# Five projection pairs of a hybrid decoder layer moved to Strassen products behind the values' stage

## The chip, the cores and the metric

The kernel runs on one core of a Trainium2 chip. The metric is the device time of one execution, in microseconds (us), taken as the median over runs; lower is better. TensorE is called PE in the profile, VectorE DVE, ScalarE ACT, GpSimd POOL and SyncE SP.

## The reference

One decoder layer works on 1024 tokens of width 1024, all in float32. The part that the change touches is the first projection and what consumes it:

```python
h = rms_norm(x, pre_mix_g[l])
proj = h @ w_in[l]
qa, ka, va, qb, kb, vb, gates = jnp.split(proj, split_at, axis=-1)
qa = apply_rope(qa.reshape(b, s, A_HEADS, 2, A_QK_DIM), cos_a, sin_a)
ka = apply_rope(ka.reshape(b, s, A_HEADS, 2, A_QK_DIM), cos_a, sin_a)
...
oa = diff_attention(qa, ka, va, lam)
...
qb = apply_rope(qb.reshape(b, s, B_GROUPS, B_HEADS, B_HEAD_DIM), cos_b, sin_b)
...
g_a, g_b = jnp.split(jax.nn.sigmoid(gates), 2, axis=-1)
mix = (g_a * ya + g_b * yb) @ w_mix_out[l]
x = x + rms_norm(mix, post_mix_g[l])
```

Attention A has 4 heads; each has two 64-wide queries and keys and is causal over all tokens (a difference of two softmaxes). Attention B has three groups of four 128-wide heads over dilated windows. The rotation of a head (`apply_rope`) takes `t1*cos - t2*sin` and `t2*cos + t1*sin` of its two halves. There are 16 gate units of 128 columns. A convolution-gated MLP follows, with two more large matrix products.

## The kernel before, in words

**Numbers.** Every float32 operand is kept as a high part (rounded to `fp32r`) and a low part (the rest). `split` (L148) makes them: ACT copies the high part (L149), DVE subtracts it from the source (L146, in `sub`). A product is three matmuls, high x high, low x high and high x low (`mm3`, L153 to L157), 128 rows deep, 128 columns of the stationary operand wide and at most 512 moving columns.

**Stages.** The transposed input stands in SBUF as `xh` and `xl` (8 blocks of 128 rows, 1024 tokens). First come the values of A and B (L445 to L653), as tokens x 2048 columns, by Strassen's scheme with seven products; sums of x are made for it (`t2`, `t3`, `t4`, and a sum that takes the place of the second half of x's first four blocks, `b12`). While the last products run, that half of x is loaded again and split (`again`, L650 to L653). The values go to DRAM through the POOL queue (`put_v`, L535). Beside it the rotation tables are made and stored in DRAM, with the row norm multiplied into them.

Then attention A begins (L907). `proj_t` (L235) projects 128 columns: it loads a unit of weights (`load_unit`, L129: two pieces of 256 KB on the SP queue, each split), and for each half of the tokens does 8 x 3 matmuls into one PSUM bank. For queries and keys the evacuation is `rotated` (L679): ACT copies the swapped blocks (L684), DVE multiplies by the two tables and adds (L685 to L687); then ACT and DVE write the high and low parts that attention uses (L730 to L744). For a gate it is `put_gate` (L248): DVE multiplies by the row norm, and the ACT queue stores it. Before head 0, one gate and head 0's projections run by themselves (L910, L911).

A head of A is eight jobs (`attend_a`, L749), one for each 128 queries: score matmuls, a minimum on DVE (L770), exponentials on ACT (L777), their difference on DVE, and later transposes (L697) and products with the values (L710, L713). Beside the jobs run *fills*: `A_FILLS` gives a string for each head, where `g` is a gate, `p` the two projections of the next A head, `P` those of the first B head, `v`, `w`, `x` and `V` loads and splits of values. `interleave` (L294) places pieces of them between the jobs by weight. Attention B (L1124) runs 12 steps of four jobs with the next step's projections as the fill, the last step with three gates (`B_GATES`). Then come the output projections, the mixing, and the MLP, whose first product is Strassen's as well (`seven`, L1437).

**Order.** Each engine and each DMA queue (SP, ACT, POOL) works in order. The order in which an engine gets its instructions is chosen by a list scheduler, from the order of the program, priorities (`tc.high_priority`) and a simulated time line; `tc.issue_after` fixes an order where it is written. Buffers are reused in turn: 18 slots of 4 KB a partition (`SLOTS`) for attention operands, six pairs of weight buffers (`slot_w`), PSUM in pools `acc` (3 banks), `pt` (2), `ps_s` (2) and `ps_o` (1).

Of the kernel before, what the change touches and what calls it, by code (L numbers as in the profile page):

```python
# [15 lines left out]
F32 = mybir.dt.float32  # L16
# [8 lines left out]
P = 128  # L25
# [24 lines left out]
START_GATES, A_FILLS, B_GATES = 1, ("gpgg", "gpvgg", "wgpgg", "xgPVgg"), 3  # L50
# [37 lines left out]
def trunk(ctx: ExitStack, tc: tile.TileContext, a, out):  # L88
# [64 lines left out]
    def mm3(o, sh, sl, mh, ml, first, last, on=False):  # L153

        nc.tensor.matmul(o, sh, mh, start=first, stop=False, skip_group_check=on)  # L155
        nc.tensor.matmul(o, sl, mh, start=False, stop=False, skip_group_check=on)  # L156
        nc.tensor.matmul(o, sh, ml, start=False, stop=last, skip_group_check=on)  # L157
# [42 lines left out]
    def halves():  # L200
        return [slice(i * 512, (i + 1) * 512) for i in range(2)]
# [20 lines left out]
    c_d = dram.tile([NF, P, S], F32, name="c_d")  # L222

# [32 lines left out]
    due, clock, marks = [], [0], {}  # L256

    @contextmanager
    def behind_marks():

        with ExitStack() as stack:
            for ins in marks.values():
                stack.enter_context(tc.issue_after(ins))
            yield

# [48 lines left out]
    rstd_row = open_pool(attn, "row", side="right").tile([P, S], F32, name="rstd_row")  # L314
    st_a = ExitStack()
# [4 lines left out]
    t2, t3, t4 = ([xw0.tile([P, 4, 512], F32R, tag=n + p, name=n + p) for p in "hl"] for n in ("t2", "t3", "t4"))  # L320
    tb = open_pool(st_v, "tb", side="right")
# [12 lines left out]

    def new_tabs():
        return [tabs.tile([P, S], F32, tag=t, name=t) for t in ("cos", "sin")]
# [17 lines left out]
    def load_tabs(first, n):  # L354

        cos, sin = new_tabs()
        for q in range(P // n):
            to = slice(q * n, (q + 1) * n)
            dma(cos[to], tab_d[0][first : first + n])
            dma(sin[to], tab_d[1 if q % 2 else 2][first : first + n])  # L360
        return cos, sin

# [11 lines left out]
    def sums_x(k, low, high):  # L374


        g1, g2 = gpre[:, k : k + 1], gpre[:, k + 4 : k + 5]
        e, o = (tb.tile([P, 2, 512], F32, tag=t, name=t) for t in ("sin", "cos"))
# [17 lines left out]
    def norm_x(m):  # L396
# [5 lines left out]
        if m < 8:  # L402
            rows_x.append(tb.tile([P, S], F32, tag=("kk", "ang", "sin", "cos")[m % 4], name="rows"))
            nc.gpsimd.dma_start(rows_x[m], a["x"][m * P : (m + 1) * P])
# [40 lines left out]
    with ExitStack() as st_y:  # L445
# [17 lines left out]
        def more_tags():  # L463

            for tag in itertools.cycle(("ang", "kk", "sin", "cos")):
                t = tb.tile([P, S], F32, tag=tag, name="raw")
# [145 lines left out]
        made, fetched, again = 12, 14, []  # L612

        places_y = {("p6", 1): (1, "a0", yv), ("p5", 1): (3, "b3", yw), ("p4", 1): (2, "b2", yw)}
        quarter.update({(q, 0): new_y(f"b{q}", yw) for q in range(1, 4)})
        for n in range(8, len(steps_v)):
# [15 lines left out]
            if n == ANGLES_AT:  # L632
                pos = [load_raw(a["positions"][sl].partition_broadcast(P), next(tags)) for sl in halves()]
                args = [tb.tile([P, S], F32, tag=n_, name=n_) for n_ in ("sin", "cos")]
# [10 lines left out]
            step_v(n)  # L645
            if k == 3 and i and p in ("p1", "p7", "p4", "p3"):
                put_v({"p1": 0, "p7": 3, "p4": 2, "p3": 1}[p], 1, p == "p1")
            if (p, i) == ("p5", 1):

                again.append(load_raw(a["xT"][k][:, 512:], next(tags)))  # L650
            if (p, i) == ("p6", 1):
                with behind_marks():
                    split_x(k, halves()[1], again[k])  # L653
    st_v.close()
    tabs = open_pool(attn, "tabs", side="right")
    cos_a, sin_a = load_tabs(64, 32)
# [22 lines left out]
    def rotated(ps, cos, sin, sl, quarter):  # L679
        t1 = rt.tile([P, 512], F32, tag="t1", name="t1")  # L680
        t2 = rt.tile([P, 512], F32, tag="t2", name="t2")
        for q in range(P // quarter):
            src, dst = slice((q ^ 1) * quarter, ((q ^ 1) + 1) * quarter), slice(q * quarter, (q + 1) * quarter)
            nc.scalar.activation(t1[dst], ps[src], AF.Copy)  # L684
# [41 lines left out]
    def proj_a(h, res):  # L726
# [3 lines left out]
        def put_q(half, sl, ps):  # L730
            t = rotated(ps, cos_a, sin_a, sl, 32)
# [5 lines left out]
        def put_k(half, sl, ps):  # L737
            t = rotated(ps, cos_a, sin_a, sl, 32)
# [8 lines left out]
        yield from proj_t(KA + h * P, put_k)  # L747

    def attend_a(h, i, ops, vs, out_sb, pair):  # L749
# [51 lines left out]
        def add(b):  # L801
            if b == 0:
                po.append(psum(F32, ps_o, "o")[:, : 2 * P].rearrange("p (n q) -> p n q", n=2))
# [50 lines left out]
    free_gates = list(range(2 * KC))  # L854
# [11 lines left out]

    def proj_b(g, h, res, between=None):
# [5 lines left out]
        def put(hi, lo):  # L873
            def evacuate(half, sl, ps):
                t = rotated(ps, *tabs_b, sl, 64).rearrange("p (i r) -> p r i", r=dil)
# [31 lines left out]
    with st_a:  # L907
        ops = [[] for _ in range(AH)]
        vs = [[] for _ in range(AH // 2)]
        run(gates(START_GATES)[0])  # L910
# [3 lines left out]
        for h in range(AH):  # L914
# [3 lines left out]
                "p": lambda: (proj_a(h + 1, ops[h + 1]), 8),  # L918
# [3 lines left out]
                "P": lambda: (proj_b(0, 0, ops_b[steps[0]]), 8),  # L922
# [27 lines left out]
    def attend_b(g, h, jj, ops, vs, sbs):  # L950
# [48 lines left out]
        def values():  # L999
            po = psum(F32, ps_o, "o")[:, : 2 * P].rearrange("p (j q) -> p j q", j=2)  # L1000
# [697 lines left out]
def layout(inp):  # L1698
# [10 lines left out]
    us = []  # L1709
    for c in plan():  # L1710
        us.append(units(w[:, c : c + P], KC, P))
# [31 lines left out]
```

## Time and profile before

| | |
|---|---|
| median of 3 runs | 1696.49 us (1695.46 to 1696.99) |
| the profiled execution | 1697.3 us, span 1695.3 us from its first to its last instruction |
| granted TensorE clock | 0.998 of full speed |
| values' stage | to about 162 us |
| gate and head 0's projections | 162 to 203 us |
| attention A | 203 to about 530 us (its minima on DVE, L770, from 208 to 503) |
| attention B | to about 875 us (its minima, L975, from 545 to 854) |
| output projections, mixing, the MLP's first plain units | to about 1117 us |
| MLP, up, by Strassen products | to about 1476 us |
| MLP, down | to the end |

How to read it: the page gives the share of the span in which each engine was busy, the chain of work that ended last, and groups of instructions by line, with the busy time, the mean duration of one in ns, and the idle time in front of them. Matmuls are pipelined, so that the durations of neighbours overlap. A line can be that of a helper. Windows give the busy time of each engine in a stretch of the span, with the number of instructions, the clock granted, the busy share of the 16 DMA engines and their rate.

### The profile page before, as it was taken

The numbers are of one execution on the slowest core, as the hardware profiler recorded it, in microseconds if no ns is written. First come the engines' busy times: TensorE is split into PE (matmuls) and PEld (weight loads), VectorE is DVE, ScalarE is ACT, GpSimd is POOL, SyncE is SP. The second block draws the span as 40 slices with busy tenths as digits, with TensorE's granted clock in tenths as the row PEclk, the third lists the DMA queues.
The fourth block names the chain that finished last, engine by engine and source line by source line (L and its number), as shares of the span: only waits on it lengthen the run. The fifth ranks groups of instructions, "written<-read, shape, count | busy, mean of one in ns | idle before, by whom it ended". The sixth has DMA issues, their size and how long they took to land.

```text
span 1695.3 us, 22960 instructions
## 1 busy us (share of the span) xinstructions
PE 1682.1 (99%) x8078; PEld 1410.0 (83%) x8078; DVE 1333.5 (79%) x2445; ACT 891.8 (53%) x1663; POOL 106.3 (6%) x174
## 2 busy tenths in 40 slices
PE   9999999999999999999999999999999999999997
PEld 7888888888888888888888888888888888888886
DVE  8795686877776766677756865899999989799967
ACT  7643575656454776666653533464444445355453
POOL 0031000000000000000123400300000000000000
PEclk9999999999999999999999999999999999999999
DMA  8677311214112213233585631132222222296524
GB/s 266 234 253 235 99 60 62 86 59 119 50 63 81 70 53 108 86 112 119 200 285 186 203 118 63 38 106 92 95 81 75 98 83 88 95 343 214 193 75 161
DMA packets 104451, 216.41 MB, mean 128 GB/s; under 512 B 12992, under 2 KB 22144, under 8 KB 104336
## 3 DMA queue, kind: packets, MB, share of 16 engines
q1 hardware_dynamic: 89296, 171.28, 30.5%
q0 software_dynamic: 10288, 35.28, 6.1%
q10 hardware_dynamic: 4752, 8.39, 1.3%
q8 instruction: 63, 1.03, 0.3%
q14 instruction: 52, 0.43, 0.1%
HBM read 167.05 MB, written 47.86 MB: 127 GB/s over the span
## 4 chain that ended last, share of the span: by engine, by line
PE 97%; DMA 2%; DVE 1%; ACT 1%; issue 0%; SPq 0%; DVEq 0%
PE acc L155 22%; PE acc L156 22%; PE acc L157 22%; PE acc L1578 3%; PE acc L1579 3%; PE acc L1577 3%; PE o L710 2%; PE pt L697 2%; PE acc L1258 2%; PE acc L1256 2%; PE acc L1257 2%; PE o L713 1%; PE s L156 1%; PE s L157 1%; PE s L155 1%; PE s L768 1%
## 5 line engine op out<-in xcount | busy, mean ns | idle before, releaser
L156 PE MATMUL acc<-xh,wlo 128*128 128x512 f32 x768 | 303.2, 395 | 0.0
L157 PE MATMUL acc<-xl,whi 128*128 128x512 f32 x768 | 303.1, 395 | 0.0
L155 PE MATMUL acc<-xh,whi 128*128 128x512 f32 x768 | 303.0, 395 | 0.0
L149 ACT ACTIVATE whi<-raw 128x512 fp32r<-128x512 f32 (+1 forms) x252 | 156.1, 626 | 170.3 <-PE acc L157 88.1
L146 DVE TENSOR_TENSOR wlo<-raw,whi 128x512 fp32r<-128x512 f32 (+1 forms) x252 | 178.8, 717 | 40.4 <-ACT whi L149 34.7
L156 PEld LDWEIGHTS acc<-xh,wlo 128*128 128x128 f32 x768 | 144.4, 188 | 27.8
L157 PEld LDWEIGHTS acc<-xl,whi 128*128 128x128 f32 x768 | 144.5, 188 | 27.5
L155 PEld LDWEIGHTS acc<-xh,whi 128*128 128x128 f32 x768 | 144.4, 188 | 27.3
L155 PE MATMUL acc<-mh,whi 128*128 128x512 f32 x400 | 155.8, 390 | 0.3 <-ACT mh L149 0.3
L156 PE MATMUL acc<-mh,wlo 128*128 128x512 f32 x400 | 155.6, 389 | 0.0
L157 PE MATMUL acc<-ml,whi 128*128 128x512 f32 x400 | 155.3, 389 | 0.0
L684 ACT ACTIVATE t<-acc 64x512 f32<-64x512 f32 (+1 forms) x160 | 94.7, 592 | 55.3 <-PE acc L157 53.3
L1454 DVE TENSOR_TENSOR u<-acc,u 128x512 f32<-128x512 f32 x133 | 91.3, 691 | 20.3 <-PE acc L157 20.1
L149 ACT ACTIVATE whi<-s 128x512 fp32r<-128x512 f32 x76 | 46.9, 627 | 102.3 <-PE acc L157 88.1
L685 DVE TENSOR_TENSOR t<-acc,cos 128x512 f32<-128x512 f32 x64 | 44.1, 690 | 67.1 <-ACT t L684 63.5
L155 PEld LDWEIGHTS acc<-mh,whi 128*128 128x128 f32 x400 | 75.1, 188 | 16.0 <-ACT mh L149 0.5
L156 PEld LDWEIGHTS acc<-mh,wlo 128*128 128x128 f32 x400 | 75.1, 188 | 15.6
L157 PEld LDWEIGHTS acc<-ml,whi 128*128 128x128 f32 x400 | 75.1, 188 | 15.5
L1578 PE MATMUL acc<-whi,wlo 128*128 128x512 f32 x220 | 77.6, 390 | 0.0
L1577 PE MATMUL acc<-whi 128*128 128x512 f32 x220 | 76.4, 389 | 0.0
L1579 PE MATMUL acc<-wlo,whi 128*128 128x512 f32 x220 | 73.2, 390 | 0.0
L777 ACT ACTIVATE s<-s,mx 128x896 f32<-128x896 f32 (+7 forms) x64 | 49.4, 772 | 36.9 <-DVE mx L770 21.0
(387 smaller groups left out, 3941.6 us busy)
## 6 DMA issues: line engine op xcount, KB each, us to landing
raw<-in_w_in SPq DMA_DIRECT2D x96, 256.0 KB, 2.9
raw<-in_w_up SPq DMA_DIRECT2D x88, 256.0 KB, 2.8
raw<-in_w_v SPq DMA_DIRECT2D x71, 256.0 KB, 4.7
raw<-c_d SPq DMA_DIRECT2D x48, 256.0 KB, 3.8
c_d<-c SPq DMA_DIRECT2D x22, 512.0 KB, 2.7
raw<-in_w_down SPq DMA_DIRECT2D x37, 256.0 KB, 4.1
v_d<-yv POOLq DMA_DIRECT2D x32, 256.0 KB, 4.5
gt_d<-gate ACTq DMA_DIRECT2D x32, 256.0 KB, 2.1
```

The lines of the kernel that those rows point to most:

```text
L146: eng.tensor_tensor(lo, src, hi.bitcast(F32), op=ALU.subtract)
L149: copy = nc.scalar.activation(hi, src, AF.Copy)
L155: nc.tensor.matmul(o, sh, mh, start=first, stop=False, skip_group_check=on)
L156: nc.tensor.matmul(o, sl, mh, start=False, stop=False, skip_group_check=on)
L157: nc.tensor.matmul(o, sh, ml, start=False, stop=last, skip_group_check=on)
L684: nc.scalar.activation(t1[dst], ps[src], AF.Copy)
L685: nc.vector.tensor_tensor(t2, ps, cos[:, sl], op=ALU.mult)
L777: exp = nc.scalar.activation(sc[c][:, :w], sc[c][:, :w], AF.Exp, bias=mx[:, c, 0:1], scale=-1.0, accum_out=den[:, c : c + 1])
L1454: nc.vector.tensor_tensor(to, made(p), x, op=ALU.add)
L1577: nc.tensor.matmul(banks[m], gh[:, tk], wh, start=f == 0, stop=False)
L1578: nc.tensor.matmul(banks[m], gl[:, tk], wh, start=False, stop=False)
L1579: nc.tensor.matmul(banks[m], gh[:, tk], wl, start=False, stop=f == NH - 1)
```

## The change

Ten of the 48 units of the projection are taken out of the attentions and done in a new stage between the values and attention A, in five pairs: the first B head's queries and keys, the last two gates, and the queries and keys of A's heads 1, 2 and 3. A pair is a product of 256 columns with the whole x, done as seven products of half the depth, half the columns and half the tokens, with the values' sums of x (`t2`, `t3`, `t4`, `b12`), which therefore stay longer. The reload of x's second half comes behind the last pair.

- *Weights.* Four sums of weight quarters are needed for a pair (`s1` to `s4`). They are made by DMAs on the POOL queue that add to their destination (`add_to`), started from a loaded quarter or from a negated copy by ACT. A pair's sums are begun up to two pairs ahead, its operands split one pair ahead.
- *Products.* `seven_q` runs p1, p4, p2, p6, p7, p5, p3; p2 goes on in p1's bank and p3 in p5's after these were read, and p3 of a pair is run behind p1 of the next. Eight PSUM banks of all pools are used in turn.
- *Rotation.* `rotate_q` multiplies the tile by both tables on DVE, and two accumulating DMAs add the swapped halves. For that the tables' signs lie differently (`load_tabs`, and `other` in `rotated`), and the columns of the three A heads are permuted on the host.
- *Storing.* `store_q` splits a tile and stores high and low parts in DRAM (`qk_d`); attention loads them into the slots it uses (`load_a`, `load_b`), by 12 DMAs for an A head and 4 for a B head. The gates go to DRAM as before, but unsplit from this stage.
- *Order.* `in_turn` fixes the order of ACT and DVE over this stage's blocks, from the last four steps of the values.
- *Attentions.* Fills become three gates a head for heads 0 to 3 with `l` and `L` for the loads; no gate runs before head 0; the last B step has two gates for three. The outputs' accumulator takes turns between `ps_o` and `acc` (`outs`).

```diff
-START_GATES, A_FILLS, B_GATES = 1, ("gpgg", "gpvgg", "wgpgg", "xgPVgg"), 3
+A_FILLS, B_GATES = ("glgg", "glvgg", "wglgg", "xgLVgg"), 2
+EARLY_GATES = 2
...
+    outs = itertools.cycle([lambda: psum(F32, ps_o, "o"), psum])
...
+    def in_turn():
+        with ExitStack() as stack:
+            for ins in tail.values():
+                stack.enter_context(tc.issue_after(ins))
+            last = nc.cur_bb.bb.instructions[-1]
+            yield
...
+                if ins.engine in (nc.scalar.engine, nc.vector.engine):
+                    tail[str(ins.engine)] = ins
...
+        pairs = [AH, len(plan()) // 2 - 1, 1, 2, 3]
...
+        def begin(src, scale=None):
+            t = sum_tile()
+            if scale:
+                nc.scalar.activation(t, src, AF.Copy, scale=scale)
+            else:
+                dma(t, src)
+            return t
+        def add_to(t, src):
+            nc.gpsimd.dma_start(t, src, accum_op=ALU.add)
+        def sums_a(n):
+            d11, d12, d21, d22 = quarters(n)
+            to = sums_q[n] = {"a11": load_raw(d11, "raw"), "s1": begin(d21), "a22": load_raw(d22, "t1"), "a12": load_raw(d12, "t2")}
+            to["s3"] = begin(to["s1"], -1.0)
+            to["s2"] = begin(to["a11"], -1.0)
+            add_to(to["s1"], d22)
+            add_to(to["s3"], d11)
+            add_to(to["s2"], to["s1"])
+        def sums_b(n):
+            _, d12, _, _ = quarters(n)
+            to = sums_q[n]
+            to["s4"] = begin(to["s2"], -1.0)
+            add_to(to["s4"], d12)
...
+            if n == len(steps_v) - 8:
+                with in_turn(), tc.high_priority(offset=60):
+                    sums_a(0)
...
+        def rotate_q(n, c, u):
+            if pairs[n] >= len(order) // 2 - KC:
+                nc.vector.tensor_tensor(u, u, rstd_row, op=ALU.mult)
+                return
+            sw = pq.tile([P, S], F32, tag="sw", name="sw", bufs=2)
+            nc.vector.tensor_tensor(sw, u, tab[1], op=ALU.mult)
+            nc.vector.tensor_tensor(u, u, tab[0], op=ALU.mult)
+            for src, dst in ((up_half, low_half), (low_half, up_half)):
+                add_to(u[dst], sw[src])
+        def store_q(n, c, u):
...
+            hi, lo = (pq.tile([P, S], F32R, tag=t, name=t, bufs=2) for t in ("qkh", "qkl"))
+            split(hi, lo, u)
...
+                for b in range(4 if head < AH else 0):
+                    to = (b % 2 * 2 + b // 2) * 32
+                    dma(qk_d[2 * head + c, i, to : to + 32], f32(t[b * 32 : (b + 1) * 32]))
...
+        for n in range(len(pairs)):
+            made_q = seven_q(n, ws_q.pop(n))
+            if n == 2:
+                tab = load_tabs(64, 32)
+            next(made_q)
+            if n:
+                next(before)
+                with in_turn():
+                    rotate_q(n - 1, 1, old[1])
+            with in_turn():
+                if n == 0:
+                    sums_a(1)
+                    sums_b(1)
+                put_w(n + 1, "a11")
+                for m, fn in ((n + 1, sums_b), (n + 2, sums_a)) if n else ((2, sums_a),):
+                    if m < len(pairs):
+                        fn(m)
+            next(made_q)
+            with in_turn():
+                if n:
+                    rotate_q(n - 1, 0, old[0])
+                put_w(n + 1, "a22", "a12")
...
+                put_w(n + 1, "s2", "s3")
...
+            old = next(made_q)
...
+                put_w(n + 1, "s1", "s4")
+                if n:
+                    store_q(n - 1, 0, last[0])
...
-        run(gates(START_GATES)[0])
         run(proj_a(0, ops[0]))
```

In `seven_q`, where `made(p, bank)` does one product's 12 matmuls:

```diff
+            m1 = made("p1")
+            copy(c11, m1)
+            yield
+            m4 = made("p4")
+            made("p2", m1)
+            m6 = made("p6")
+            add(c12, m6, c11)
+            copy(c11, m1)
+            yield
+            m7 = made("p7")
+            add(c22, m7, c12)
+            add(c21, m4, c22)
+            yield
+            m5 = made("p5")
+            add(c22, m5, c22)
+            yield us
+            made("p3", m5)
+            add(c12, m5, c12)
```

More of the change, by code (lines that the diff above doesn't have):

```diff
@@ L677, in split_values, with rotated @@
                 split(*res[-1], v)
-    def rotated(ps, cos, sin, sl, quarter):
+    def rotated(ps, cos, sin, sl, quarter, other=()):
         t1 = rt.tile([P, 512], F32, tag="t1", name="t1")
@@ L865, in trunk, with load_b @@
     tabs_b, wk_b = [], []
+    def load_b(g, h, res):
+        ops = [slot(n) for n in ("qh", "ql", "kh", "kl")]
+        res += ops
+        at = where[QB + g * 512 + h * P]
+        for n, t in enumerate(ops):
+            dma(f32(t), qk_d[at + n // 2, n % 2])
     def proj_b(g, h, res, between=None):
```

157 lines of the change are left out of this document (122 added, 35 removed).

## The prediction

> **What bounds the kernel now.** I read the page's engine shares and its chain first, then who TensorE waits for.
>
> ```profile
> span 1695.3 us, 22960 instructions
> PE 1682.1 (99%) x8078; PEld 1410.0 (83%) x8078; DVE 1333.5 (79%) x2445; ACT 891.8 (53%) x1663; POOL 106.3 (6%) x174
> ...
> PE 97%; DMA 2%; DVE 1%; ACT 1%; issue 0%; SPq 0%; DVEq 0%
> ```
> ```profile
> PE acc L155 <- ACT xh L371: 1.8, 2, 1.4
> PE pt L578 <- DVE t4l L575: 1.2, 1, 1.2
> PE acc L155 <- ACT mh L149: 0.3, 1, 0.3
> ```
>
> The chain is 97% TensorE, and TensorE's waits add up to 3.3 us, most of it before the first products. So a TensorE instruction that goes is worth its full issue interval, and everything else costs nothing until it makes TensorE wait. The interval isn't the listed mean of a matmul: those overlap. Windows restricted to the tile acc give it, and windows over all engines the load of each stage.
>
> ```profile
> 162.00:203.00 41.00, 40.77 (x180) 33.80 (x180) 4.15 (x6) 9.88 (x17) 1.00 0.41 128
> ```
> ```profile
> 90.00:128.00 38.00, 38.00 (x173) 31.52 (x172) 37.27 (x71) 13.76 (x22) 13.81 (x23) 1.00 0.83 288
> 128.00:162.00 34.00, 34.00 (x151) 28.16 (x150) 19.98 (x31) 13.56 (x23) 4.86 (x9) 1.00 0.70 218
> 203.00:280.00 77.00, 77.00 (x386) 65.20 (x385) 59.10 (x132) 47.86 (x96) 0.00 (x0) 1.00 0.21 72
> 1130.00:1480.00 350.00, 350.00 (x1546) 289.91 (x1545) 318.04 (x426) 150.23 (x203) 3.38 (x34) 1.00 0.26 88
> ```
>
> The columns are window, length, then busy time of PE, PEld, DVE, ACT and (where it works) POOL, the granted clock, DMA share, GB/s. From 162 to 203 us (a gate and head 0's projections) 180 matmuls of 512 columns take 40.77 us: 0.2265 us each, at full clock. The last row matters too: in the feed-forward Strassen stage DVE works 318 of 350 us, 91%, and TensorE is busy throughout.
>
> **Matmuls removed.** Each 128-column projection is 2 halves x 8 k x 3 = 48 matmuls, a pair 96. Strassen takes 7 products x 4 k x 3 = 84. Five pairs (a B head, two gates, A heads 1 to 3) lose 12 each: 60 x 0.2265 = 13.6 us. The other matmuls, transposes included, stay. So a new pair lasts 84 x 0.2265 = 19.0 us on TensorE, a product 2.72, the five pairs 95.1.
>
> **What the new stage asks of DVE and ACT.** Rows by form, the mean in ns behind the comma:
>
> ```profile
> L146 DVE TENSOR_TENSOR wlo<-raw,whi 128x512 fp32r<-128x512 f32 x250 | 178.0, 719 | 37.5 <-ACT whi L149 31.9 <-DMA sin<-tab_d 2.7 <-POOL gl L1225 1.2
> L149 ACT ACTIVATE whi<-raw 128x512 fp32r<-128x512 f32 x250 | 155.3, 628 | 169.4 <-PE acc L157 88.1 <-issue 22.8 <-PE acc L1578 13.3
> L1454 DVE TENSOR_TENSOR u<-acc,u 128x512 f32<-128x512 f32 x133 | 91.3, 691 | 20.3 <-PE acc L157 20.1
> L1343 DVE TENSOR_TENSOR c<-c 128x1024 f32<-128x1024 f32 x22 | 26.9, 1224 | 0.1
> L146 DVE TENSOR_TENSOR vl<-vperm,vh 128x1024 fp32r<-128x1024 f32 x16 | 19.4, 1222 | 2.6 <-ACT vh L149 2.6
> L149 ACT ACTIVATE vh<-vperm 128x1024 fp32r<-128x1024 f32 x16 | 16.5, 1048 | 0.1
> ```
>
> A head's pair costs DVE 7 weight splits (7 x 0.719 = 5.0), 5 additions out of PSUM (3.5), 4 multiplications by the tables (4 x 1.224 = 4.9) and 2 splits for storing (2.4): 15.8 of 19.0 us, 83%. ACT: 7 splits 4.4, two copies 1.2, three negated copies 1.9, two stores 2.1: 9.6 us. The gate pair asks less. This is below the 91% that costs nothing at 1130 to 1480 us, so I price it at zero. If that cover fails it is because DVE or ACT, which work in order, stand waiting for a DMA; that is priced next.
>
> **The accumulating DMAs.** The trace has none. Per head's pair the change puts 8 on the POOL queue: four for weight sums (s1, s3, s2, s4; s2 waits for s1, s4 for s2) and four for the rotation (two per tile). Nearest are the plain 256 KB transfers from the same queue, at the busiest place of the kernel, and the weight loads.
>
> ```profile
> L535 POOL DMA_DIRECT2D v_d<-yv x32: 540/541/902, 107.2 to 163.9; - x32
> DMA to landing us min/median/max: 2.7/4.5/8.3
> ```
> ```profile
> raw<-in_w_v SPq DMA_DIRECT2D x71, 256.0 KB, 4.7
> ```
>
> Let L be the time from issue to landing. Below, the plain one: 2.7 to 4.5 us. Above, twice the plain one, because a destination has to be read as well: 9 us at the median, 16.6 at the slowest. Less than nothing is excluded, as these DMAs replace no transfer on TensorE's path. I take 7 to 9, nearer to twice the median, since the stage is as full of transfers as 90 to 128 us. Three places feel L.
> - Pair 0. Its sums are issued eight steps (8 x 2.72 = 22 us) before the values end, and s4 is used 6 products later: no wait at any L up to about 10.
> - Pair 1. Its sums begin about when pair 0 does. s2 is ready at 4.7 + 2L + 1.3 (load, two accumulations, split) and is used after ten products, at 27.2. TensorE waits 2L - 21: nothing at 9, 12 us at 16.6. Behind ACT's waiting negation of s2 queue later splits, so I take 1 us at L = 8.
> - Stores of a rotated tile. DVE's and ACT's order is fixed by hand here, so a store that waits for its rotation holds everything behind it: the next pair's negated copies, and through them the POOL queue, which in turn waits for s1 before the next rotation. That loop lasts about 2L + 4 us (two landings, issues and copies) against 19.0: free up to L = 7.5. It closes only once, while pair 1 is multiplied, since pair 2's slot has the gates, which have no rotation, and the last two slots begin no new sums. At L = 8 to 9 it costs 1 to 3 us; I take 1.5.
>
> **Bytes.** A head's pair moves 7 weight pieces, one sum to another, 4 rotations and 2.1 MB of stored high and low parts: 20 pieces of 0.262 MB, 5.2 MB in 19 us, or 275 GB/s. The row of 90 to 128 us carried 288 with TensorE never idle, and the page's slices of 42 us go up to 343:
>
> ```profile
> GB/s 266 234 253 235 99 60 62 86 59 119 50 63 81 70 53 108 86 112 119 200 285 186 203 118 63 38 106 92 95 81 75 98 83 88 95 343 214 193 75 161
> ```
>
> Counted over all five pairs (the gates' has 12 pieces), tables (2.1) and the reload of x (1.0), 27 MB go into 95.1 us plus the 21.7 of head 0's projections (96 x 0.2265) that follow: 234 GB/s. So bytes alone don't bind; they make L long. [...]
>
> **What only moves.** The reload and split of x's second half (four pieces of SP's, eight operations like a split, 5.4 us on two engines) goes behind the last p5; it is awaited by the second half of head 0's queries, one product and 24 matmuls later, 8.2 us: nothing, and if its cover is gone 1 or 2 us once. The tables' loads come earlier on SP, the first during pair 0, whose rotation is a pair later. POOL's mask for A stands behind the accumulations, but is wanted only after head 0's projections: nothing.
>
> **The attention of A.** What leaves each of the windows like 203 to 280: two units, 96 matmuls, 21.7 us of TensorE, with their DVE work of 4 splits (2.9), 12 rotation operations and 12 splits of 64 rows:
>
> ```profile
> L685 DVE TENSOR_TENSOR t<-acc,cos 128x512 f32<-128x512 f32 x64 | 44.1, 690 | 67.1 <-ACT t L684 63.5 <-PE pt L697 2.0 <-PE o L713 1.3
> L744 DVE TENSOR_TENSOR l<-t,k 64x512 fp32r<-64x512 f32 x32 | 21.9, 684 | 1.0 <-ACT k L741 0.4
> ```
>
> 12 x 0.690 + 12 x 0.684 + 2.9 = 19.4 us. So DVE goes from 59.1 of 77 (77%) to 39.7 of 55.3 (72%): attention alone isn't denser on DVE than before. What is lost is filling: 3 gates behind eight jobs, where there were 3 gates and 2 projections. Bounds: a gain of 1 us (the second accumulator bank for the outputs) to a loss of 3 us a head; I take 0.5 in all, as the gates depend on nothing and can be placed anywhere. The twelve loads a head (3.1 MB in 55 us, 57 GB/s on top of 72) sit on SP's queue ahead of the next gate's weights and wait for slots that the head before has left by then: nothing. With two gates for three, the last B step keeps 21.7 us of filling: nothing.
>
> **Sum.** -13.6 + 1 + 1.5 + 0.5 = -10.6 us. The profiled execution took 1697.3 us, 2.0 more than its span; that gives 1686.7. The median of the runs, 1696.5, is 0.8 lower: 1685.9, say 1686.
>
> **Rivals.**
> [...]
> - *Attention runs dry.* If a head's chain (scores, DVE's minimum, exponentials, transposes) shows through with less filling, at 2 us a head: 8 us instead of 0.5, with the rest 1693.5. Against: DVE at 72% only.
> - *Slower: the POOL queue.* If L passes about 12.5, the three places together cost what was saved: pair 1 waits 4, the loop 10. At the upper bound 16.6: pair 1 12 us, the loop 18, two late stores 3 each, about 36 less a few that overlap, 30: 1696.5 - 13.6 + 30 = 1713. For: the queue works in order and nothing here shows an accumulation. Against: 4.5 us at the median with DVE 37.27 of 38 us busy. [...]
> - *It doesn't do what it says.* Should matmuls be kept, their count wouldn't fall; the loop bounds leave little room.
>
> **How the numbers follow.** About 0.2% (3.4 us) is what a measurement of this kernel can tell from no change: faster is below 1693.1, slower above 1699.9. Forecast (1682.5 to 1690) 0.64; transfers bind 0.13, half of it below 1693.1; attention dry 0.07, a little more than half below; slower 0.12; the rest, 0.04, no change. Faster: 0.64 + 0.065 + 0.045 = 0.75; slower 0.12; same 0.13. The range starts at 1682, all gain and a little more, and runs to 1699: the two middle rivals are inside, about 0.12 are above and some 0.06 below.
>
> **What would show it.** TensorE's count 60 lower, and its total shorter by 13 to 14 us of matmul intervals. In the new stage TensorE's idle should be 1 to 4 us, behind ACT's or DVE's splits near the start of pairs 1 and 2; accumulations land at 7 to 9 us; DVE stands at about 83%. A head's attention lasts 55 us. I am wrong if accumulations land later than 12 us, if the DMA share in the stage is 0.95 and TensorE waits for weight splits all through it, or if a head lasts more than 58 us.

## The result and the profile after

The kernel after takes 1753.88 us (median of 4 runs, 1749.96 to 1759.28), the kernel before 1696.74 us beside it (4 runs): a ratio of 1.0339, with a 95% interval of 1.0309 to 1.0368. It is 57 us slower where 10.6 us of gain were forecast. The profiled execution took 1759.3 us, the longest of the four and 62.0 more than that of before. The page of after:

```profile
span 1757.5 us, 23054 instructions
PE 1695.6 (96%) x8018; PEld 1412.0 (80%) x8018; DVE 1334.9 (76%) x2419; ACT 864.9 (49%) x1615; POOL 138.3 (8%) x210
PEclk9999999899999999999999999999999999999999
PE 77%; DMA 9%; DVE 6%; issue 3%; ACT 3%; POOL 1%; SPq 1%; DVEq 0%; ACTq 0%; POOLq 0%
```

The 60 matmuls are gone (8078 to 8018), but TensorE no longer ends the chain alone: its share fell from 97% to 77%. Three numbers give the whole difference. TensorE is idle for 1757.5 - 1695.6 = 61.9 us, before 1695.3 - 1682.1 = 13.2: 48.7 more. Its busy time grew by 13.5 us although 13.6 us of matmuls went, so the rest takes 27.1 us longer; the mean granted clock fell from 0.998 to 0.984, and 1.4% of 1696, my estimate of the clock's part, is 24 of them. 48.7 + 27.1 - 13.6 = 62.2, the difference of the spans. Who TensorE waits for:

```profile
PE pt L898 <- DVE s L993: 13.9, 10, 3.4
PE s L976 <- DVE mx L979: 9.7, 10, 4.3
PE pt L156 <- DVE u L763: 8.7, 2, 6.0
PE s L156 <- DVE stat L1190: 3.2, 1, 3.2
PE acc L911 <- ACT pt L150: 2.9, 2, 1.5
```

Only the third line belongs to the new stage. The others are waits of attention A (the fourth: of B's first step) for its own softmax, which other products used to cover. Windows by stage show the same (window, length, then busy time of PE, PEld, DVE, ACT, POOL, the granted clock, DMA share, GB/s): most of the new stage, its last products and head 0's projections, the start of head 0, from the end of head 0 into head 1, from head 2 into head 3, and at the end everything from 200 to 660 us.

```profile
162.00:262.00 100.00, 93.97 (x405) 77.30 (x404) 56.50 (x73) 36.00 (x61) 25.58 (x31) 0.97 0.76 181
262.00:301.00 39.00, 35.53 (x150) 28.63 (x149) 28.94 (x40) 24.53 (x40) 4.13 (x6) 0.96 0.77 207
301.00:345.00 44.00, 27.42 (x111) 19.84 (x112) 32.99 (x79) 23.30 (x47) 0.00 (x0) 0.81 0.70 178
345.00:396.00 51.00, 50.62 (x284) 43.51 (x283) 34.16 (x106) 19.37 (x47) 0.00 (x0) 1.00 0.44 129
450.00:510.00 60.00, 55.98 (x297) 46.93 (x296) 38.50 (x116) 22.39 (x57) 0.00 (x0) 0.94 0.35 119
200.00:660.00 460.00, 419.15 (x2103) 349.75 (x2102) 301.71 (x726) 213.59 (x455) 17.16 (x25) 0.95 0.44 124
```

In the kernel before, TensorE was busy for all 460 us from 200 to 660, at clock 1.00. Here it stands still for 40.9 of them, and at a clock of 0.95, 5% of 419 us, 21 us more, go to the clock by the same estimate. The worst place is the start of head 0: 27.42 us of work in 44, at 0.81.

### The profile page after: what moved, and what is told of

Read it like the earlier page. It is cut to its first block, busy times and chain, and to the rows that moved or that the text cites. A ratio compares the mean times of both kernels' runs of the same rounds, so it can differ in the third digit from the quotient of the medians.

```text
span 1757.5 us, 23054 instructions
## 1 busy us (share of the span) xinstructions
PE 1695.6 (96%) x8018; PEld 1412.0 (80%) x8018; DVE 1334.9 (76%) x2419; ACT 864.9 (49%) x1615; POOL 138.3 (8%) x210
## 4 chain that ended last, share of the span: by engine, by line
PE 77%; DMA 9%; DVE 6%; issue 3%; ACT 3%; POOL 1%; SPq 1%; DVEq 0%; ACTq 0%; POOLq 0%
PE acc L156 17%; PE acc L157 16%; PE acc L158 16%; PE acc L1794 3%; PE acc L1792 3%; PE acc L1793 3%; PE acc L1471 2%; PE acc L1473 2%; PE acc L1472 2%; PE pt L898 2%; DMA raw<-in_w_in 2%; DMA mw<-e_d 1%; DMA s<-in_w_in 1%; DMA u<-sw 1%; PE acc L911 1%
## 5 line engine op out<-in xcount | busy, mean ns | idle before, releaser
L157 PE MATMUL acc<-xh,wlo 128*128 128x512 f32 x640 | 254.1, 397 | 0.0
L156 PE MATMUL acc<-xh,whi 128*128 128x512 f32 x640 | 253.9, 397 | 0.0
L158 PE MATMUL acc<-xl,whi 128*128 128x512 f32 x640 | 253.8, 397 | 0.0
L158 PEld LDWEIGHTS acc<-xl,whi 128*128 128x128 f32 x640 | 121.2, 189 | 23.6
L156 PEld LDWEIGHTS acc<-xh,whi 128*128 128x128 f32 x640 | 121.5, 190 | 23.2
L157 PEld LDWEIGHTS acc<-xh,wlo 128*128 128x128 f32 x640 | 121.4, 190 | 22.8
L150 ACT ACTIVATE whi<-s 128x512 fp32r<-128x512 f32 x96 | 58.7, 626 | 123.5 <-PE acc L158 100.7
L886 DVE TENSOR_TENSOR t<-acc,cos 128x512 f32<-128x512 f32 x48 | 33.2, 692 | 67.6 <-ACT t L885 63.9
L885 ACT ACTIVATE t<-acc 64x512 f32<-64x512 f32 (+1 forms) x104 | 61.6, 593 | 45.3 <-PE acc L158 42.7
L979 DVE CUSTOM_DVE_ANT_0 s<-s,mask_a 128x512 f32<-128x512 f32 (+3 forms) x96 | 52.3, 554 | 32.7 <-PE s L977 17.7
```

What stands on the lines that cost most here:

```text
L150: copy = nc.scalar.activation(hi, src, AF.Copy)
L158: return nc.tensor.matmul(o, sh, ml, start=False, stop=last, skip_group_check=on).ins
L885: nc.scalar.activation(t1[dst], ps[src], AF.Copy, scale=-1.0 if q in other else 1.0)
L979: nc.vector.tensor_tensor_reduce(out=s_sb[:, c0:c1], in0=ps, in1=mask, scale=-scale, scalar=3.0e38, op0=ALU.add, op1=ALU.min, accum_out=mx ...
```

## The experiments

Every kernel of this part is the change, or the kernel before, with the edit shown; `...` stands for lines that only go along with it. Times are medians, and ratios are set against the kernel before on the same chip. *Lost time* is how much further apart TensorE's matmuls start than the median interval of their shape in the kernel before, summed over a stretch; it holds idle time and a lower clock together. The first four asked what in the change slows attention A: the loads on SP's queue, the missing filling, the accumulating DMAs, or something else.

**The loads on another queue.**

```diff
-            dma(f32(to), src)
+            nc.gpsimd.dma_start(f32(to), src)
...
```

> The loads of the stored heads (12 for an A head, 4 for the B head) are issued from the POOL queue instead of SP's; nothing else changes. Theory S (SP's queue): these loads keep the gates' weights back, so that attention A has no other matmuls beside it; then TensorE's idle time from attention A's first scores to B's first (about 32 us after the change) falls below 10, and the kernel takes about 1725 us. Theory F (filling): twelve pieces of filling a head are too few beside eight jobs whatever the loads do; then the idle time stays within 5 us of what it is and the kernel at 1748 to 1758.

Measured: 1762.36, ratio 1.0384 (1.0368 to 1.0399). The loads no longer stand ahead of the gates' weights on SP, and nothing is gained; the time is 4 us above even the case in which filling is what lacks. The queue isn't the main cause.

**Two pairs instead of five, the old filling in A.**

```diff
-A_FILLS, B_GATES = ("glgg", "glvgg", "wglgg", "xgLVgg"), 2
+A_FILLS, B_GATES = ("gpgg", "gpvgg", "wgpgg", "xgLVgg"), 2
...
-        pairs = [AH, len(plan()) // 2 - 1, 1, 2, 3]
+        pairs = [AH, len(plan()) // 2 - 1]
...
```

> Only the first B head and the two gates go by Strassen's scheme; the projections of A's heads 1 to 3 are again fills of attention A, as before the change. Saves 24 matmuls, 5.4 us. S and F both: attention A has its filling and its weights again, so its idle time goes to under 3 us, and the time is 1691 plus what the new stage still stalls (the one rotation behind a full POOL queue, 3 to 8 us): 1694 to 1700. If the loss in attention A comes from something else that the change brought (outputs in two accumulator banks, other places in SBUF), over 20 us of idle time stay there, 1715 or more.

Measured: 1750.16, ratio 1.0313 (1.0297 to 1.0328). Heads 0 to 2 have the two projections back and A's heads load nothing, yet nearly the whole loss stays. So neither the filling nor the loads decide as long as the rest of the change is there; what is left of it in A is the outputs' second bank.

**The rotation without accumulating DMAs**, by ACT copies and a DVE addition.

```diff
-            nc.vector.tensor_tensor(sw, u, tab[1], op=ALU.mult)
+            for src, dst in ((up_half, low_half), (low_half, up_half)):
+                nc.scalar.activation(sw[dst], u[src], AF.Copy, scale=-1.0)
+            nc.vector.tensor_tensor(sw, sw, tab[1], op=ALU.mult)
             nc.vector.tensor_tensor(u, u, tab[0], op=ALU.mult)
-            for src, dst in ((up_half, low_half), (low_half, up_half)):
-                add_to(u[dst], sw[src])
+            nc.vector.tensor_tensor(u, u, sw, op=ALU.add)
```

> The rotation in the new stage without accumulating DMAs: ACT copies the swapped halves (two copies of 64 rows a tile), DVE adds once more. Theory R: the stage's idle time (9.5 us from 162 to 301 us) is the store that waits for the accumulated rotation; then it falls below 2 us and the kernel is 8 to 12 us faster, 1742 to 1746. Rival: the sums of weights, which still accumulate, cause it; then idle time stays at 7 or more. S and F: attention A keeps its loss of about 30 us of idle time either way.

Measured: 1759.59, ratio 1.0372 (1.0355 to 1.0389). The stall at 203 us is gone, but another stands at 262 us, before the first weights of head 0's projections:

```profile
PE acc L156 <- ACT whi L150: 6.0, 1, 6.0
```

**The gates back from the stage into A** (one more in head 0 and one in head 1: 16 pieces in each, a piece being 12 matmuls).

```diff
-A_FILLS, B_GATES = ("glgg", "glvgg", "wglgg", "xgLVgg"), 2
-EARLY_GATES = 2
+A_FILLS, B_GATES = ("glggg", "glvggg", "wglgg", "xgLVgg"), 2
+EARLY_GATES = 0
...
-        pairs = [AH, len(plan()) // 2 - 1, 1, 2, 3]
+        pairs = [AH, 1, 2, 3]
```

> The two gates go back from the new stage into attention A, one each to heads 0 and 1, whose filling rises from 12 to 16 pieces; everything else as after the change. Costs 12 matmuls more, 2.7 us. F: the idle time of heads 0 and 1 (about 20 us) falls by half or more, and with the colder clock that goes with it the kernel is about 10 us faster, 1744. S: the gates come late whatever their number; idle time falls by less than 4 us and the kernel stays within 4 us of 1754.

Measured: 1759.0, ratio 1.0365 (1.0342 to 1.0388). More gates bring nothing while the outputs use two banks.

**One bank for the outputs**, with the change otherwise kept; the same with the rotation on the engines; the same with the loads on POOL's queue.

```diff
-    outs = itertools.cycle([lambda: psum(F32, ps_o, "o"), psum])
+    outs = itertools.cycle([lambda: psum(F32, ps_o, "o")])
```

> The change with one thing undone: the attentions' output accumulator stays in its own bank (ps_o) instead of taking turns with the three banks of the projections. Theory O (banks): a bank taken in turn by an output is held until its last product, and the gates, whose halves take the three banks in turn, can't run ahead of attention; so attention A stands bare at the beginning of each head even with the old filling. Then TensorE's idle time from A's first scores to B's first falls from about 32 us to under 5, the clock goes back up, and the kernel takes 1700 to 1712 us. If O is wrong the time stays within 1746 to 1758.

> One output bank, and the rotation by ACT copies and DVE instead of accumulating DMAs. O with theory R (rotation): as the kernel with one bank alone, less the stage's stall for a rotated tile, 5 to 8 us. R's rival, as the run with this rotation alone suggested (the stage's idle time only moved to its end): no faster than one bank alone within 4 us.

> One output bank, and the stored heads loaded over the POOL queue. S in a weak form (the loads delay gates' weights at head 0 only): up to 6 us faster than one bank alone. If SP's queue doesn't matter: within 3 us of it.

Measured: 1735.76, 1738.0 and 1737.12, ratios 1.0237 (1.022 to 1.0254), 1.0236 and 1.0229. The first lies between the two cases expected: the bank is worth 18 us here, and much of the loss is something else. Rotation and queue are worth nothing beside it either. Windows of the first of the three:

```profile
345.00:520.00 175.00, 175.00 (x938) 150.30 (x937) 114.17 (x319) 73.61 (x174) 0.00 (x0) 1.00 0.36 109
520.00:580.00 60.00, 51.52 (x260) 43.98 (x259) 47.55 (x156) 33.35 (x81) 0.00 (x0) 0.77 0.19 66
```

For 175 us, most of heads 0 to 2, TensorE is busy without a gap, with three gates a head. Then filling is used up: from 540 to 560 us not one matmul of a projection starts, and in the 60 us around it idle and clock take, by the same estimate, 8.5 + 0.23 x 51.5 = 20 us.

**Only the second bank, in the kernel before.**

```diff
+    outs = itertools.cycle([lambda: psum(F32, ps_o, "o"), psum])
...
-                po.append(psum(F32, ps_o, "o")[:, : 2 * P].rearrange("p (n q) -> p n q", n=2))
+                po.append(next(outs)()[:, : 2 * P].rearrange("p (n q) -> p n q", n=2))
...
```

> The kernel before with that part of the change alone: outputs take turns between ps_o and the projections' banks. O: attention A and B stall as after the change, 30 to 50 us slower than before, 1727 to 1747. If O is wrong: within 4 us of before, 1693 to 1701.

Measured: 1736.7, ratio 1.0233 (1.0218 to 1.0248). As expected of the banks, this one part of the change, alone, costs 39.7 us, with all the old filling in place.

**Two output banks of their own, and seven banks.** In the kernel before, `acc` is cut to two banks until the attentions and A's output projection end; in the first run the outputs have two of their own, in the second one, and a bank is left empty.

```diff
-    acc = open_pool(ctx, "acc", bufs=3, space=PSUM)
+    accs = [open_pool(attn, "acc", bufs=2, space=PSUM)]
...
-    ps_o = open_pool(attn, "ps_o", space=PSUM)
+    ps_o = open_pool(attn, "ps_o", bufs=2, space=PSUM)
...
```

> The kernel before, unchanged but for the banks: outputs have two banks of their own, the filling's products two instead of three. Two outputs in two banks by turns cost the kernel before 39.7 us when the second was one of the filling's three. If what costs is the turn-taking (an output that is held over several jobs sits in the ring from which the filling takes its next bank, and makes it wait), two banks each should give most of it back: within 8 us of the kernel before. If what costs is that the filling has two banks left, it stays near 1737. If outputs that run ahead of the order they had are themselves the harm, it stays near 1737 too, and the run with seven banks tells the two apart.

> The kernel before with one output bank and two banks for the filling (the eighth is left empty in the attentions). If a third bank matters to the filling, this is slower by 10 to 40 us; if not, it is within 5 us of the kernel before, and then neither the number of the filling's banks nor their size is what the second output bank costs.

Measured: 1709.01, ratio 1.0071 (1.0056 to 1.0086), and 1710.68, ratio 1.008 (1.0065 to 1.0095). The first is 12 us above the kernel before, a little more than turn-taking was to leave, and the second, 14 us above, falls in the case that a third bank matters to the filling; but the place decides between them. TensorE's matmuls into the tile acc alone, at the start of head 0: with the shared bank,

```profile
203.00:240.00 37.00, 14.53 (x60) 0.86 0.16 55
```

and with two banks each:

```profile
203.00:240.00 37.00, 33.72 (x141) 1.00 0.17 60
```

The kernel before has 140 there. With turn-taking the filling simply stops; in the 20 us from 220 no projection matmul starts, where 73 did. What it stops for shows in the order of TensorE's work with the shared bank:

```profile
217.99 0.39 PE L157 MATMUL acc<-xl,whi 128*128 128x512 f32 x1
...
244.28 0.34 PE L711 MATMUL acc<-pt,vh 128*128 128x256 f32 x1
244.46 0.40 PE L155 MATMUL acc<-xh,whi 128*128 128x512 f32 x1
```

The second line is the first product of the output that sits in `acc`. The filling goes on right behind it, and 11 us before that output is read out (255.5 us). The same follows at 328.6 and 412.3 us, and in the change itself at 341.4 and 403.5. So the filling doesn't wait for the output to be finished but for it to begin; and to begin it needs the scores, softmax and transposes that the filling should have covered. Whether the ring of banks or the scheduler's order enforces this isn't shown.

With separate banks the filling runs as before, and all 337 us to 540 are idle-free; with the shared one they are not (TensorE's busy time in the run with two banks each, then in the run with the shared bank):

```profile
203.00:540.00 337.00, 337.00 (x1762) 1.00 0.22 74
203.00:540.00 337.00, 317.34 (x1595) 0.96 0.19 64
```

What the two runs lose, they lose later, at the passage to B (4 and 6 us of lost time from 540 to 580) and in B's output projections (6 and 4 us from 925 to 945):

```profile
PE acc L156 <- DVE gl L1225: 4.1, 1, 4.1
```

There `acc` has its three banks again, so a lack of banks isn't shown to be the cause; it stays open.

So of the 39.7 us at least 28 (1736.7 - 1709.0) are the turn-taking. By the lost time it is nearly all: 39 us stand from 203 to 540 us with the shared bank, 2 in the kernel before and 2 in either run with rings of their own, and what these two lose later the run with the shared bank doesn't lose. That the outputs themselves gain from a second bank isn't seen: 1709.0 against 1710.7, with overlapping intervals.

**The B head's projections back to head 3**, with one bank, and the same with the loads put last in the fills.

```diff
-A_FILLS, B_GATES = ("glgg", "glvgg", "wglgg", "xgLVgg"), 2
+A_FILLS, B_GATES = ("glgg", "glvgg", "wglgg", "xgPVgg"), 2
...
-        pairs = [AH, len(plan()) // 2 - 1, 1, 2, 3]
+        pairs = [len(plan()) // 2 - 1, 1, 2, 3]
...
```

> One output bank, and the first B head's projections go back from the new stage into head 3's filling, as before the change; four pairs are left (the gates, A's heads 1 to 3), 48 matmuls saved, 2.7 us less than five. Theory F' (filling runs out): with one bank the twelve pieces a head are enough for heads 0 to 2, and only head 3's end, where nothing follows that could be taken forward, stands bare; then the lost time around the last head (24 us above nominal matmul intervals, half of it a colder clock) falls to under 6 and the kernel takes 1712 to 1719. If the last head's loss isn't filling it stays and the time is 1736 to 1740.

> As the run with four pairs, with the loads of the next A head put behind the head's gates in the program's order. Theory S at head 0: 7 to 10 us of loss there come from weights that stand on SP's queue behind sixteen loads of heads 1 and 2; then it is 5 to 9 us faster than the run with four pairs. If head 0's loss is the bytes under way (stores, tables, values at 0.7 of the DMA engines), within 3 us of it.

Measured: 1721.56, ratio 1.014 (1.0122 to 1.0157), and 1722.14, ratio 1.0147 (1.013 to 1.0164). The first is 14.2 us better than one bank alone although 12 matmuls (2.7 us) came back, yet short of what was expected. The end of A, where 20 us were lost, is nearly whole:

```profile
520.00:580.00 60.00, 58.19 (x310) 49.71 (x309) 45.60 (x116) 35.54 (x75) 1.59 (x4) 0.97 0.17 58
```

The second gained nothing: twelve loads and two of values still stand ahead of the gates' weights on SP, and the stall as head 0 begins is 6.1 us there. In the first it is 8.1 us, and the reason is on ACT's time line: it stands 12 us before a split, behind a weight that SP issued after 16 loads, with the exponentials and DVE's part queued behind it.

```profile
307.47 0.63 ACT L150 ACTIVATE whi<-raw 128x512 fp32r<-128x512 f32 x1 [12.08 <-DMA raw<-in_w_in]
```

**Those weights first.** A head's loads are held behind the weights on SP, and head 0 gets four gates.

```diff
-A_FILLS, B_GATES = ("glgg", "glvgg", "wglgg", "xgPVgg"), 2
+A_FILLS, B_GATES = ("ggggl", "gvggl", "wggl", "xgPVgg"), 2
...
+        with tc.issue_after(last_raw[-1].ins):
```

> One output bank, the B head's projections back in head 3, and the loads of the next head held on the SP queue behind the weights of the head's fourth gate piece. The run without this order took 1721.6, with a stall of 8.1 us at the start of head 0, where ACT waits 12.1 us for a weight piece that SP issued behind 16 loads. If the SP queue's order makes that stall, it goes: 1712 to 1716. If it is the bytes under way there, the piece lands late all the same: 1719 to 1724.

Measured: 1725.18, ratio 1.0168 (1.0151 to 1.0185). The four loads of head 2 no longer stand ahead, but those of head 1 still precede a weight piece that ACT needs: SP issued it at 294.46 instead of 299.84 us, and it landed 6.9 us later, where the same kind of piece takes 2.9 at the median of 96 in the kernel before. ACT waits again:

```profile
301.45 0.63 ACT L152 ACTIVATE whi<-raw 128x512 fp32r<-128x512 f32 x1 [6.91 <-DMA raw<-in_w_in]
```

The stall is 5.4 us instead of 8.1, but from 460 to 500 us the lost time is 11.5 us where it was 7.6, and the whole comes out just above even the slower case expected. In both stalls the DMA engines are full, first in the run with four pairs, then in this one (a share can pass 1, since a transfer counts where it starts):

```profile
285.00:308.00 23.00, 15.65 (x70) 12.31 (x68) 7.61 (x19) 4.70 (x8) 0.00 (x0) 0.93 0.94 235
285.00:304.00 19.00, 13.60 (x61) 10.95 (x61) 7.95 (x19) 5.40 (x9) 0.00 (x0) 0.93 1.04 288
```

Order and bytes both seem to have a part in the stall, then, and the run doesn't separate them. This stays open.

**The gates spread otherwise**, five pairs, one bank.

```diff
-A_FILLS, B_GATES = ("glgg", "glvgg", "wglgg", "xgLVgg"), 2
+A_FILLS, B_GATES = ("glg", "glvgg", "wglg", "xgLVgggg"), 2
```

> One output bank, all five pairs, and A's twelve gates spread as 2, 3, 2 and 5 over the heads instead of 3 each. F' with the total enough: the last head's loss falls by half or more and the kernel takes 1718 to 1726. F' with the total too small: the loss moves to an earlier head and the time stays within 5 us of 1736.

Measured: 1737.84, ratio 1.0234 (1.0219 to 1.025), as with one bank. The scheduler draws on the fills when it can, so their sum counts and not the string of a head.

**Only gate pairs in the stage**, one bank, projections in the attentions as before: one, three and two pairs (20, 16, and in the mean 18 pieces a head). The strings are those below for one pair; "gpg", "gpvg", "wgpg", "xgPVg" for three; and the first two of these with the last two of those for two.

```diff
-A_FILLS, B_GATES = ("glgg", "glvgg", "wglgg", "xgLVgg"), 2
+A_FILLS, B_GATES = ("gpgg", "gpvgg", "wgpgg", "xgPVgg"), 2
...
-        pairs = [AH, len(plan()) // 2 - 1, 1, 2, 3]
+        pairs = [len(plan()) // 2 - 1]
...
```

> One output bank, the new stage with the pair of gates alone, all of attention's filling as before the change: no rotation, no stored heads, 12 matmuls (2.7 us) saved. All theories: the losses in the attentions are gone. The stage itself then costs what its beginning and end stall: 1694 to 1698. If its beginning stalls without any rotation, 1699 to 1706.

> One output bank; three gate pairs and no other in the stage (no rotation, no accumulating DMA for one); heads 0 to 3 keep their projections as filling and have two gates each instead of three: 16 pieces a head where the version with one gate pair had 20 and the change 12. 36 matmuls fewer, 8.2 us. If the stage costs its 3 to 4 us at its ends once, whatever its length, and 16 pieces are enough to cover the jobs, 1692 to 1694: faster than the kernel before. If 16 pieces are already too few, a head loses 2 to 4 us: 1700 to 1708.

> As the run with three gate pairs, but with two: heads 0 and 1 have two gates and two projections (16 pieces), heads 2 and 3 three gates and two projections (20 pieces). 24 matmuls fewer, 5.4 us. The run with three pairs lost 12 us at 400 to 440 (head 2) and 14 us from 540 to 610 (the end of head 3 and the start of B). If each head lives on its own filling, both losses go with the gates that came back there: 1693 to 1696. If the scheduler takes filling wherever it can and the sum over the heads counts, half of the loss stays: 1702 to 1708.

Measured: 1698.87, ratio 1.0009 (1.0 to 1.0018); 1715.37, ratio 1.0109 (1.0093 to 1.0124); 1711.45, ratio 1.0082 (1.0065 to 1.0098). The first, just above what was expected, loses its 2.7 us again; 1.4 of that is a wait for the pair's last addition as the stage ends. The other two lie above even the slower case expected: nothing there rotates or loads a head, only the sums of weights still accumulate (12 transfers and 8), and the more is saved on matmuls, the slower it gets. With 20 pieces a head, a window in A:

```profile
380.00:460.00 80.00, 80.00 (x423) 68.34 (x422) 62.62 (x163) 45.51 (x96) 0.00 (x0) 1.00 0.27 86
```

and with 16:

```profile
380.00:460.00 80.00, 73.86 (x375) 61.57 (x374) 62.31 (x166) 50.04 (x107) 0.00 (x0) 0.94 0.24 76
```

With two pairs the loss at 380 to 420 stays (11.5 us of lost time) and so does the one at the passage to B (7.2 us from 580 to 620), although heads 2 and 3 have their 20 pieces: once more the sum counts. In this kernel the limit lies between 18 and 20 pieces a head in the mean. No version tried beats the kernel before.

## Why the prediction was wrong

- *Matmuls removed.* Right by count: 60 fewer. Their 13.6 us can't be read off by themselves, since the rest of TensorE's busy time grew by 27.1 us, of which the clock explains 24 by the estimate above.
- *The failed step* is the one on attention A: "Bounds: a gain of 1 us (the second accumulator bank for the outputs) to a loss of 3 us a head; I take 0.5 in all, as the gates depend on nothing and can be placed anywhere." For this 0.5 the trace of the change has 57 us of lost time from 300 to 660 us, and the minima of the four heads run from 309 to 546 us, 59 us a head where over 58 was to show me wrong. Gates depend on a PSUM bank and its turn. When the outputs take turns in the ring of three from which the filling takes its banks, the filling waits until an output has begun, and with it for the very chain that it should cover. Alone that is 39.7 us; in the change, which has less filling to lose, taking it out gives 18.1.
- *The same step, second half: what is lost is filling.* I compared DVE's share, 72% against 77%, and called attention no denser. But filling doesn't cover DVE's mean load; it covers the chain of each job, which is as long as before. The rival that runs dry had the mechanism, at 8 us and with DVE's load as the argument against it. Measured: 16.9 us for the B head's pair at the end of A (14.2, and 2.7 of matmuls), and 27 us where 4 pieces a head were taken for three gate pairs (1715.37 - 1696.79 + 8.2; some 4 of them are the stage's own, as with one gate pair).
- *The loads on SP's queue.* I had priced nothing for them. As a main cause they fell, but at head 0's start they stand ahead of the gates' weights and fill the DMA engines, and there is the stall of 8.1 us with one bank and the B head back. The last B step with two gates wasn't tried by itself.
- *The new stage.* I forecast 1 to 4 us of idle; from 162 to 301 us it is 9.5. The store that waits for its rotation was the right place. It waits for its accumulations on ACT:

```profile
204.75 1.06 ACT L150 ACTIVATE qkh<-u 128x1024 fp32r<-128x1024 f32 x1 [10.41 <-DMA u<-sw]
```

  DVE's additions stand behind it, and through them, not through the POOL queue as in my loop, TensorE:

```profile
209.12 0.79 PE L156 MATMUL pt<-xh,whi 128*128 128x512 f32 x1 [6.03 <-DVE u L763]
```

  The size was off: 6.0 and, at 265.9 us, 2.6 us for the 1.5. It closes twice. At the first the tiles' four accumulations landed after 8.8 to 11.6 us, at the second after 3.5 and 5.5, and there it is the rotation that comes late. Curing it alone gains nothing, as the engine rotation showed: the weights behind are late as well. DVE's load wasn't the limit: it was busy 56.5 of the 100 us from 162.
- *The accumulating DMAs.* All 36, by the line that issues them:

```profile
L652 POOL DMA_DIRECT2D u<-sw x16: 802/956/1720, 191.2 to 277.8; - x16
L652 POOL DMA_DIRECT2D s<-in_w_in x15: 850/893/1492, 137.1 to 235.3; - x15
L652 POOL DMA_DIRECT2D s<-s x5: 852/861/907, 143.6 to 221.2; - x5
DMA to landing us min/median/max: 3.3/5.8/11.6
```

  and the plain ones of the same queue and run, from the page:

```profile
v_d<-yv POOLq DMA_DIRECT2D x32, 256.0 KB, 4.9
```

  5.8 us at the median, near the plain 4.9, where I had taken 7 to 9. So a landing isn't doubled. The time of the DMA engines is, nearly. From 166 to 290 us of the change, packets, MB and share of the 16 engines' time, first the plain transfers on SP's queue, then POOL's, which are 32 of the accumulations:

```profile
q1 hardware_dynamic: 6196, 15.12, 39.4%
q0 software_dynamic: 3584, 8.39, 39.9%
```

  For the same time the accumulations move little more than half the bytes (8.39 MB against 15.12). What makes it so isn't shown.

  The POOL rival falls: no landing took over 11.6 us where it needed more than 12.5, and an issue takes 0.8 to 1.7 us, above the 0.54 of a plain one in the kernel before.
- *Bytes.* Over the stage the DMA share was 0.76 at 181 GB/s, so transfers don't bind it on the average, as forecast. But the mean hides the place of the first stall, where they do:

```profile
190.00:210.00 20.00, 13.97 (x60) 11.30 (x59) 8.03 (x11) 5.42 (x10) 6.35 (x8) 0.93 1.02 235
```

  The engines are full there at 235 GB/s, less than the 288 that 0.83 of them carried at 90 to 128 us in the kernel before. With the rotation on ACT and DVE they are as full in the same 20 us (1.01, at 294 GB/s), but no store waits for an accumulation and TensorE is busy for 19.4 of them. So full transfers cost where a store waits for one. That transfers bind, to which I gave 0.13, holds for this stretch; over the whole stage, at a share of 0.76, it isn't shown.
- *The accounting by runs.* The change loses 57.1 us net, 70.7 before its saving. The bank gives 18.1, the B pair 16.9, the three A pairs 30.9 (1721.56 - 1698.87 + 8.2), and 4.2 stay for a stage with one gate pair: 70.1. Steps in a row must add up nearly, so that the sum is no test, and in another order the sizes would differ (the bank alone is 39.7). How the 30.9 divide is told only by the traces, not by runs of their own: against the run with one gate pair, the one with four pairs loses some 7 us more from 232 to 300 us (the stage and head 0's projections), 11 from 300 to 345 (head 0's start) and 16 from 450 to 660 (heads 2 and 3 and the passage to B, filling again), and about 2 less elsewhere.

## What to carry to other kernels

Work that runs beside a latency-bound chain is not free to move because it is independent: count the pieces that cover each job, and take away no more than the trace shows to be spare, which an idle-free TensorE doesn't tell. Give an accumulator that waits for such a chain a bank of its own, never one of the ring that its own cover draws from. Read the share of the DMA engines where a wait stands, not over the stage. And a matmul saved in front of such a chain is worth its interval only as long as the chain stays covered.

## What the runs showed of the hardware

In the run with one bank, where filling had run out, TensorE was not only idle but also slower:

```profile
520.00:530.00 10.00, 8.97 (x57) 1.00 0.58 209
530.00:540.00 10.00, 7.82 (x28) 0.64 0.07 28
540.00:550.00 10.00, 8.96 (x39) 0.51 0.00 0
```

The first and the last stretch are both 90% busy, but the last has half the clock and two thirds of the matmuls. TensorE is idle for 1.0 us in each of these two and for 2.2 us in the one between, so the clock fell beside little idle time; what lowers it isn't shown. By the sums of the result each microsecond of idle cost about one and a half in the change (48.7 us more of idle came with 27.1 of slower matmuls, 24 of them by the clock, an estimate from 0.998 and 0.984), and no term of my sum, all taken at full clock, could have held it.
